# Two heads' value products merged, attention-weight remainders added by DMA, and the orders around them, in a two-layer encoder kernel

## The chip, the cores and the metric

The kernel runs on one core of one Trainium2 chip. The metric is the time of one execution on the device in microseconds. Three runs of the kernel before gave 1129.76, 1130.61 and 1131.30 us, median 1130.61 us.

The engines are named as in the profile: PE multiplies matrices (PEld loads its weights beside it), DVE and ACT work on tiles of 128 partitions and read PE's PSUM banks, POOL works on tiles in SBUF and can issue DMAs that add to what stands at the destination, SP issues the other DMAs.

## The reference, cut to what matters

Two layers over a sequence of 512 tokens with 1024 features, in float32. Layer 0 mixes tokens with latent attention (16 heads), layer 1 with an mLSTM (4 heads); behind each stands an FFN with 4096 hidden features.

```python
x += mla(rmsnorm(x));    x += ffn(rmsnorm(x), 0)
x += mlstm(rmsnorm(x));  x += ffn(rmsnorm(x), 1)

def mla(h):                                  # 16 heads
    cq  = rms_norm(h @ w_dq)                 # 512 x 384
    ckv = rms_norm((h @ w_dkv)[:, :256])     # 512 x 256, and 32 rotary columns
    q, k, v = cq @ w_uq, ckv @ w_ukv, ...    # per head 96 + (64 and 64)
    return softmax(mask(q @ k.T)) @ v @ w_o  # by heads, q and k normed, rotary

def mlstm(h):                                # 4 heads
    q, k, v, o = split(h @ w_in)             # v: 256 columns a head
    ...                                      # gates, decayed q k^T v, normed by row

def ffn(h, l): return square(relu(h @ w1[l])) @ w2[l]
```

## The kernel before, in words

**Numbers in two parts.** PE multiplies in f32r, a rounded form of float32. Every operand is therefore held as a rounded part hi and a remainder lo = raw - hi, and every product is three matmuls, hi*hi, hi*lo and lo*hi (`mm3`). A weight tile is loaded raw by DMA, ACT casts it to hi, and DVE (or POOL, or both by columns) subtracts to get lo (`split_w`, from line 155).

**Stages.** First comes `mla`. Its prologue computes the latents cq and ckv for four blocks of 128 tokens (tokens 0 to 3). The heads go in 8 pairs; each pair has one tile of weights, 128x1280 (`w_qkv`), split in `pair_w`: columns 0 to 767 on DVE, 768 to 1279 on POOL. Then follow the FFN of layer 0, the mLSTM, and the FFN of layer 1.

**What sets the order.** `ipe`, `idve`, `iact` and `ipool` keep what is issued through them in program order on their engine (all of it is recorded at line 80); what is issued through `nc.` directly, and ACT and POOL in most of `mla` and of the mLSTM, is placed by a scheduler when the kernel is built. In `mla` the program order is a list of two-letter units, written by hand. START is the prologue: W is a pair's weight split, R the transposes of a token block's latents, r their split, g, e and h the norm and the rotary part of the latents, P the product of a pair and a token block, A, B, C its squares, its scale and its scaled copy f, X the transposes of f, x their split. So "W10" is the second pair's weights and "P02" the first pair's product for token block 2. ORDER is one round of the heads in the middle, LAST the rounds of the last heads.

**The FFN.** The hidden features go in 8 chunks. A chunk's first product F gives z, squared; POOL makes four sums of z's quarters, ACT and DVE split them into hh and hl. The second product P uses seven products of sums of w2's quarters (a Strassen-Winograd form), (c,k) being chunk c and product k. The sums of the quarters are made by DMAs from POOL's queue that add to what was loaded. In the last chunk (7) all four sums t1 to t4 live in two tiles named z: `l_load` loads b12 four times, and `l_sum` (lines 804 to 806) adds b11 and b22 to t1 to t3, and b11, b22 and b21 to t4, one after another. It is called behind products k of chunk 6 (lines 936 to 942), whose order is 0, 1, 2, 3, 5, 4, 6. t4 feeds the very last product (7,6); its split is named zw. The adds of a finished product into x are DVE's `y_add`. The PSUM banks that they free are named tp. In layer 0, transposes that make the normed input xg of the mLSTM stand between the halves of the last two products; (7,5,0) and (7,5,1) are the two halves of product 5 of chunk 7.

**The mLSTM.** For each head, v is made with 256 (head 0: 264, with gates) columns a token block; the weights `w_v0`, and `w_v` for heads 1 to 3, are loaded raw in two tiles each, and those of head 0 are subtracted on POOL. `rows_sb` spreads a column of scales along the free axis: DVE writes them on diagonals, and one fp32 matmul with a matrix of ones gives the rows.

Of the kernel before, what the change touches and what calls it, by code (L numbers as in the profile page):

```python
# [16 lines left out]
F32 = mybir.dt.float32  # L17
F32R = mybir.dt.float32r
# [43 lines left out]
def trunk(ctx: ExitStack, tc, a, yT, dbg=None):  # L62
# [33 lines left out]
    def tmp(dt=F32):  # L96
        return ph[0].tile([P, 512], dt, tag="t", bufs=tb[0], name=nm("t"))
# [4 lines left out]
    def big(dt):  # L102
        return ph[0].tile([P, 4, 512], dt, tag="big", bufs=6, name=nm("big"))
# [84 lines left out]
    def rows(r):  # L188

        dg = tmp()  # L190
# [4 lines left out]
        return ps  # L195

    def rows_sb(r):
        ps = rows(r)
        R = ph[0].tile([P, T], F32, name=nm("R"))
        nc.scalar.copy(R, ps)  # L200
        return R
# [54 lines left out]
    def mla(mp):  # L256
# [101 lines left out]

        def new_pair(g):
            S = Pair()  # L360
            S.f, S.f2, S.ps, S.sps, S.tps, S.xps, S.mx = {}, {}, {}, {}, {}, {}, [None, None]
            S.p = [{}, {}]
            S.pT = [None, None]
            S.raw = load_raw(a["w_qkv"][g], PAIR_W)
            S.v = vt[g % 3]
            S.r = sp.tile([P, NB, 4], F32, tag="scr", bufs=4, name=nm("scr"))
            return S

        def pair_w(S):
            S.w = split_w(S.raw, PAIR_W, ENG[CFG[0]], ENG[CFG[1]], None if S is pairs[0] else ENG[CFG[4]], 3 * NQ,  # L370
                          [big(F32R).rearrange("p j e -> p (j e)") for _ in range(2)] if S is pairs[0] else None)

        pairs = {g: new_pair(g) for g in range(3)}
        gz = xtile()
# [206 lines left out]
        def o_split(S, h):  # L581
            o_sum(S, h)
            if h == 1:
# [4 lines left out]
                else:  # L588
# [9 lines left out]
        ORDER = ("S0 s0 P0 S1 S2 T0 X0 s1 T1 s2 D1 A0 T2 P1 M0 E0 t0 B0 t1 t2 E2 E3 A1 E1 V0 x0 X1 V1 V2 W0 V3 N0 C0 B1 x1 o0")  # L598

        START = ("W00 Z00 Z01 g00 e00 g01 Z02 R00 h00 r00 e01 Z04 g02 P00 R01 h01 A00 Z03 e02 r01 B00 W10 R02 g03 h02 C00 r02 P01 X00 A01 e03 R03 P02 B01 h03 r03 A02 C01 B02 P03 P10 x00 X01 C02 x01 A03 B03 X02 p11 x02 S01 C03 A10 P12 S00 X03 B10 W20 s01 A11 C10 X10 x03 s00 S02 A12 B11 s02 p13 M00 B12 C11 X11 x10 E00 E02 A13 B13 E01 E03 C12 N00 C13 x11")  # L600
# [122 lines left out]
    def ffn(fp, layer, last):  # L723
# [181 lines left out]
        for s_ in range(2, len(units) - 2):  # L905
# [80 lines left out]
    def mlstm(lp):  # L986
# [16 lines left out]
        def gates(gps):  # L1003
# [45 lines left out]
            nc.vector.tensor_scalar_mul(cs, r, DK ** -0.5)  # L1049
            G["cs"] = cs  # L1050

        for h in range(MH):
            nv = DV + (2 * MH if h == 0 else 0)
            src = a["w_v0"] if h == 0 else a["w_v"][h - 1]
            ws = [load_w(src[c], 4 * nv, nc.gpsimd if h == 0 else nc.vector) for c in range(2)]
            vh, vl = vt[2 * (h % 2)], vt[2 * (h % 2) + 1]
            nc.gpsimd.memset(vh.bitcast(F32)[:, :, DV:], 1.0)
            nc.gpsimd.memset(vl.bitcast(F32)[:, :, DV:], 0.0)
            gps = []
            for t in range(NB):  # L1060
# [7 lines left out]
                if h == 0 and t == 0:  # L1068
# [139 lines left out]
def _layout(i):  # L1208
# [13 lines left out]
    def rows_by_two(w):  # L1222
# [31 lines left out]
    o["w_v"] = np.stack([np.stack([cols(wv[:D // 2, h * DV:(h + 1) * DV]), cols(wv[D // 2:, h * DV:(h + 1) * DV])])  # L1254
                         for h in range(1, MH)])
# [24 lines left out]
```

## Time and profile before

| what | value |
|---|---|
| runs of before | 1129.76, 1130.61, 1131.30 us (median 1130.61) |
| the profiled execution | 1130.33 us, its span 1128.6 us |
| PE busy | 1107.3 us (98%) |
| DVE busy | 763.3 us (68%) |
| ACT busy | 568.0 us (50%) |
| POOL busy | 363.4 us (32%) |
| PE's longest waits | 2.4 us (for DVE's add into x), 1.9 us twice, 1.6 us |

The span is what the trace covers; the profiled execution's own time is 1.7 us longer. Shares of busy time are means over stages with different limits. PE's busy time is the sum of modelled spans of pipelined matmuls, so the distance between the starts of equal matmuls tells more than their duration. The granted clock, PEclk, is 1.00 at PE's 2.4 GHz and 0.50 at 1.2 GHz. A row's bracket gives the idle time of its engine just before it and what ended it.

### The profile page before, as it was taken

What the parts mean: (1) busy time and instruction counts of PE and PEld (TensorE: products, weight loads), DVE (VectorE), ACT (ScalarE), POOL (GpSimd) and SP (SyncE); (2) the same over time, 40 slices, a digit from 0 to 9 for tenths busy, and PEclk for the clock granted to TensorE, in tenths of its full rate; (3) what the DMA queues carried; (4) which work ended last, traced back from release to release, by engine and by line L of the source; (5) the groups of instructions that cost most, each with busy time, mean ns of one, the idle gap of its engine ahead of it and who ended that gap; (6) DMA issues with size and microseconds to landing.
All of it is one profiled execution on the core that took longest, in us unless ns stands there. A gap on an engine that the chain in (4) does not pass through costs nothing.

```text
span 1128.6 us, 15807 instructions
## 1 busy us (share of the span) xinstructions
PE 1107.3 (98%) x5790; PEld 949.1 (84%) x5790; DVE 763.3 (68%) x1308; ACT 568.0 (50%) x1004; POOL 363.4 (32%) x481
## 2 busy tenths in 40 slices
PE   9899999999999999999999999999999999999998
PEld 8889988888888888888798898888888888888876
DVE  5689997455676776776776465554476776767567
ACT  4478876437444544444465344332654545444442
POOL 3567785203332323324330011000323224224250
PEclk9899999999999999999999999999999999999999
DMA  9201021455666676575923223222675575666575
GB/s 323 72 25 48 20 76 38 131 170 127 170 151 149 165 154 146 151 174 149 203 71 102 86 58 92 81 90 81 197 170 130 159 180 131 164 168 139 160 153 127
DMA packets 44669, 146.23 MB, mean 130 GB/s; under 512 B 4912, under 2 KB 8368, under 8 KB 44592
## 3 DMA queue, kind: packets, MB, share of 16 engines
q1 hardware_dynamic: 34512, 108.52, 30.6%
q0 software_dynamic: 10080, 36.70, 19.2%
q8 instruction: 46, 0.75, 0.3%
q14 instruction: 31, 0.25, 0.1%
HBM read 143.11 MB, written 2.10 MB: 129 GB/s over the span
## 4 chain that ended last, share of the span: by engine, by line
PE 90%; DMA 3%; DVE 3%; POOL 2%; ACT 1%; issue 1%; SPq 0%; ACTq 0%; DVEq 0%; POOLq 0%
PE mm L80 40%; PE tp L80 34%; PE mm L178 4%; PE mm L177 4%; PE mm L176 4%; PE po L80 3%; DMA z<-in_w 1%; DMA wr<-in_w_z 1%; DVE x L80 1%; PE tp L178 1%; PE tp L177 1%; PE tp L176 1%; DMA t<-in_x 1%; POOL z L80 0%; POOL x L80 0%
## 5 line engine op out<-in xcount | busy, mean ns | idle before, releaser
L80 PE MATMUL mm<-xg,wh 128*128 128x512 f32 (+1 forms) x1088 | 318.9, 377 | 0.0
L80 POOL TENSOR_TENSOR z<-z 128x256 f32<-128x256 f32 x128 | 145.1, 1153 | 348.3 <-ACT z L80 345.8
L80 PEld LDWEIGHTS mm<-xg,wh 128*128 128x128 f32 x1088 | 200.1, 188 | 37.5
L80 PE MATMUL mm<-xg,wl 128*128 128x512 f32 (+1 forms) x544 | 204.9, 377 | 0.0
L80 DVE TENSOR_TENSOR wl<-tw,wh 128x1024 fp32r<-128x1024 f32 x104 | 134.5, 1293 | 87.9 <-ACT wh L80 87.9
L80 PE MATMUL tp<-wh,hh 128*128 128x512 f32 x424 | 165.3, 390 | 4.7 <-DVE x L80 4.7
L80 PE MATMUL tp<-wh,hl 128*128 128x512 f32 x424 | 165.0, 389 | 0.0
L80 PE MATMUL tp<-wl,hh 128*128 128x512 f32 x424 | 165.0, 389 | 0.0
L80 DVE TENSOR_TENSOR wl<-wr,wh 128x1024 fp32r<-128x1024 f32 (+1 forms) x72 | 94.0, 1306 | 102.1 <-ACT wh L80 102.1
L80 DVE SCALAR_TENSOR_TENSOR x<-tp,r,x 128x512 f32<-128x512 f32 (+1 forms) x223 | 155.2, 735 | 2.6 <-PE tp L80 2.5
L80 ACT ACTIVATE t<-mm 128x512 f32<-128x512 f32 (+3 forms) x97 | 54.3, 559 | 185.5 <-PE mm L80 179.5
L80 ACT CAST wh<-tw 128x1024 fp32r<-128x1024 f32 x104 | 108.9, 1047 | 40.5 <-DMA tw<-in_w 23.7
L80 PEld LDWEIGHTS mm<-xg,wl 128*128 128x128 f32 x544 | 102.4, 188 | 18.9 <-DVE wl L80 0.4
L80 PEld LDWEIGHTS tp<-wh,hh 128*128 128x128 f32 x424 | 79.6, 188 | 22.6 <-issue 3.5
L80 ACT CAST wh<-wr 128x1024 fp32r<-128x1024 f32 (+1 forms) x74 | 79.0, 1067 | 29.9 <-PE tp L80 25.5
L80 PEld LDWEIGHTS tp<-wh,hl 128*128 128x128 f32 x424 | 79.6, 188 | 16.6
L80 PEld LDWEIGHTS tp<-wl,hh 128*128 128x128 f32 x424 | 79.6, 188 | 16.5
L80 POOL DMA_DIRECT2D tw<-in_w x56 | 49.1, 876 | 124.4 <-DVE wl L80 112.4
L166 DVE TENSOR_TENSOR wl<-wr,wh 128x1024 fp32r<-128x1024 f32 (+1 forms) x39 | 45.7, 1173 | 56.3 <-ACT wh L162 55.5
L162 ACT CAST wh<-wr 128x1024 fp32r<-128x1024 f32 (+2 forms) x42 | 41.9, 1001 | 63.1 <-PE mm L177 31.6
L80 ACT ACTIVATE hh<-z 128x1024 fp32r<-128x1024 f32 x32 | 34.0, 1064 | 71.5 <-POOL z L80 71.5
L80 PE MATMUL mm<-wh,big 128*128 128x256 f32 (+1 forms) x256 | 58.2, 306 | 0.0
(286 smaller groups left out, 2096.5 us busy)
## 6 DMA issues: line engine op xcount, KB each, us to landing
wr<-in_w SPq DMA_DIRECT2D x64, 512.0 KB, 3.7
tw<-in_w SPq DMA_DIRECT2D x62, 512.0 KB, 4.2
tw<-in_w POOLq DMA_DIRECT2D x56, 512.0 KB, 5.7
z<-in_w POOLq DMA_DIRECT2D x14, 512.0 KB, 7.7
wr<-in_w_qkv SPq DMA_DIRECT2D x8, 640.0 KB, 3.9
wr<-in_w_oa SPq DMA_DIRECT2D x8, 512.0 KB, 3.6
z<-in_w SPq DMA_DIRECT2D x8, 512.0 KB, 7.3
wr<-in_w_mo SPq DMA_DIRECT2D x8, 512.0 KB, 3.6
```

What stands on the lines that cost most here:

```text
L80: return lambda *args, **kw: tc.keep_in_program_order(f(*args, **kw)) if self.on else f(*args, **kw)
L162: act.copy(hi[:, :n], raw[:, :n])
L166: dve.tensor_sub(lo[:, :n], raw[:, :n], hi[:, :n].bitcast(F32))
L176: pe.matmul(out, lhsT=lh, rhs=rh, start=start, stop=False)
L177: pe.matmul(out, lhsT=lh, rhs=rl, start=False, stop=False)
L178: pe.matmul(out, lhsT=ll, rhs=rh, start=False, stop=stop)
```

## The change

It does six things.

1. Pairs 3 to 7 of the attention weights: ACT writes lo as the negated rounded weights, a DMA from POOL's queue adds the raw weights (640 KB) to it, and ACT casts hi. Pairs 0 to 2 are split as before.
2. Units are moved in START, ORDER and LAST: "W10" goes from before R02 to behind "h02 e03", P01 and P02 come ahead of R03 and X00, and W0 goes to an earlier place in two lists.
3. `l_sum`: t4's b11 is added behind the z sums and behind t2's b22, and t4's b22 behind that.
4. The remainders of `w_v0`, two subtractions of 128x1056, are made on DVE.
5. v of heads 2 and 3 is one product with 512 columns: 96 matmuls of 512 columns for 192 of 256, from four tiles of weights, in four PSUM banks.
6. `rows_sb` splits the scales into two rounded parts and uses two f32r matmuls.

```diff
     def pair_w(S):
-        S.w = split_w(S.raw, PAIR_W, ENG[CFG[0]], ENG[CFG[1]], None if S is pairs[0] else ENG[CFG[4]], 3 * NQ,
...
+        if S.g < 3:
+            S.w = split_w(S.raw, PAIR_W, iact, idve, None if S.g == 0 else ipool, 3 * NQ,
...
+            return
+        hi, lo = S.w = [wp.tile([P, WMAX], F32R, tag=n, name=nm(n)) for n in ("wh", "wl")]
+        iact.activation(lo[:, :PAIR_W], S.raw[:, :PAIR_W], AF.Copy, scale=-1.0)
+        ipool.dma_start(lo[:, :PAIR_W], a["w_qkv"][S.g], accum_op=add)
+        iact.copy(hi[:, :PAIR_W], S.raw[:, :PAIR_W])
...
-  START = ("... P00 R01 h01 A00 Z03 e02 r01 B00 W10 R02 g03 h02 C00 r02 P01 X00 A01 e03 R03 P02 B01 ...
+  START = ("... P00 R01 h01 A00 Z03 e02 r01 B00 R02 g03 r02 C00 P01 h02 e03 W10 A01 P02 R03 X00 B01 ...
...
                     elif k == 3:
-                        l_sum(("t1", "b11"), ("t2", "b11"), ("t3", "b22"), ("t4", "b11"))
+                        l_sum(("t1", "b11"), ("t2", "b11"), ("t3", "b22"))
                     elif k == 5:
                         s_load(c + 1, ("b21", "b22"))
-                        l_sum(("t2", "b22"), ("t4", "b22"))
+                        l_sum(("t2", "b22"), ("t4", "b11"))
+                    elif k == 4:
+                        l_sum(("t4", "b22"))
                     elif k == 6:
                         l_sum(("t4", "b21"))
...
-            ws = [load_w(src[c], 4 * nv, nc.gpsimd if h == 0 else nc.vector) for c in range(2)]
+                ws = [load_w(src[c], 4 * nv) for c in range(2)]
...
+            if h == 2:
+                z = [ps_mm() for _ in range(3)] + [pp.tile([P, 512], F32, tag="po", bufs=1, name=nm("po"))]
+                for j in range(4):
+                    w = load_w(a["w_v23"][j], D)
+                    for t in range(NB):
+                        for k in (2 * j, 2 * j + 1):
+                            o_mm(z[t], w, k, t, xg)
...
+    def rows_sb(r):
+        rh, rl = small(NB), small(NB)
+        nc.vector.tensor_copy(rh.bitcast(F32R), r)
+        nc.vector.tensor_sub(rl, r, rh)
+        dh, dl = tmp(F32R), tmp(F32R)
         for t in range(NB):
-            nc.vector.tensor_scalar_mul(dg[:, t * P:(t + 1) * P], ident, r[:, t:t + 1])
+            c = slice(t * P, (t + 1) * P)
+            nc.vector.tensor_scalar_mul(dh[:, c], ident, rh[:, t:t + 1])
+            nc.scalar.activation(dl[:, c], ident, AF.Copy, scale=rl[:, t:t + 1])
         ps = ps_tp()
-        pe.matmul(ps, lhsT=ones, rhs=dg, start=True, stop=True)
+        pe.matmul(ps, lhsT=ones_r, rhs=dh, start=True, stop=False)
+        pe.matmul(ps, lhsT=ones_r, rhs=dl, start=False, stop=True)
```

Three places in the engines' lists. The first is DVE's list in the prologue of `mla`, around token block 2's split, before: `wl` is the second pair's remainder, `z_ue` the latents' norm, `f` the scaled first pair of token block 0, `big` and `ck` the remainders of the turned latents of block 2, `x` the scaled latents of block 3.

```order
L80 TENSOR_TENSOR wl_587<-wr_369,wh_586 128x768
L80 TENSOR_SCALAR z_ue<-z_ms,rx_390 128x3
L80 SCALAR_TENSOR_TENSOR f_582<-mm_527,scr_368,qtab 128x128 x2
L80 TENSOR_TENSOR f_582<-mm_527,scr_368 128x2x64
L80 TENSOR_TENSOR big_214<-tp_591,big_213 128x3x128
L80 TENSOR_TENSOR big_214<-tp_592,big_213 128x128
L80 TENSOR_TENSOR ck_216<-tp_592,ck_215 128x128
L80 SCALAR_TENSOR_TENSOR x_649<-tp_222,z_ab,x_375 128x384
```

The same place now:

```order
L80 TENSOR_SCALAR z_ue<-z_ms,rx_390 128x3
L80 TENSOR_TENSOR big_214<-tp_586,big_213 128x3x128
L80 TENSOR_TENSOR big_214<-tp_587,big_213 128x128
L80 TENSOR_TENSOR ck_216<-tp_587,ck_215 128x128
L80 SCALAR_TENSOR_TENSOR f_582<-mm_527,scr_368,qtab 128x128 x2
L80 TENSOR_TENSOR f_582<-mm_527,scr_368 128x2x64
L80 SCALAR_TENSOR_TENSOR x_634<-tp_222,z_ab,x_375 128x384
L80 SCALAR_TENSOR_TENSOR x_634<-tp_222,r_388,x_375 128x32
L80 SCALAR_TENSOR_TENSOR x_635<-po_223,z_ab,x_377 128x256
L80 TENSOR_TENSOR wl_640<-wr_369,wh_639 128x768
```

The weights' remainder went from the front of this part to its end, and the split of block 2 ahead of `f`.

The second place is the last adds into x at the end of layer 0's FFN on DVE, before: `x_3191` and `x_3195` are the second feature half of token blocks 0 and 1, `zw_5869` and `zw_5886` the remainders for the products (7,5) and (7,6), `tp_5797` and `tp_5798` the two banks.

```order
L80 TENSOR_TENSOR zw_5869<-z_5649,zw_5869 128x1024
L80 SCALAR_TENSOR_TENSOR x_3191<-tp_5797,r_737_3422,x_3191 128x512
L80 SCALAR_TENSOR_TENSOR x_3195<-tp_5798,r_737_3422,x_3195 128x512
L80 TENSOR_TENSOR zw_5886<-z_5649,zw_5886 128x1024
L80 SCALAR_TENSOR_TENSOR x_3191<-tp_5817,r_737_3422,x_3191 128x512
L80 SCALAR_TENSOR_TENSOR x_3195<-tp_5818,r_737_3422,x_3195 128x512
L80 SCALAR_TENSOR_TENSOR x_3199<-tp_5797,r_737_3422,x_3199 128x512
```

The same place now, with `wl_6024` and `wl_6030`, the remainders of the two `w_v0` tiles:

```order
L80 TENSOR_TENSOR zw_5869<-z_5649,zw_5869 128x1024
L80 SCALAR_TENSOR_TENSOR x_3191<-tp_5797,r_737_3422,x_3191 128x512
L166 TENSOR_TENSOR wl_6024<-wr_6021,wh_6023 128x1056
L80 SCALAR_TENSOR_TENSOR x_3195<-tp_5798,r_737_3422,x_3195 128x512
L80 TENSOR_TENSOR zw_5886<-z_5649,zw_5886 128x1024
L166 TENSOR_TENSOR wl_6030<-wr_6027,wh_6029 128x1056
L80 SCALAR_TENSOR_TENSOR x_3191<-tp_5817,r_737_3422,x_3191 128x512
L80 SCALAR_TENSOR_TENSOR x_3195<-tp_5818,r_737_3422,x_3195 128x512
L80 SCALAR_TENSOR_TENSOR x_3199<-tp_5797,r_737_3422,x_3199 128x512
```

Two subtractions came in, the first between the adds that free the two banks. On ACT the cast of the first tile, `wh_6023`, stands right behind the cast of `zw_5886`, as before.

The third place is POOL's list there, before: `z_5646` holds t1 and t2, `z_5649` t3 and t4, `z_5642` is the last z.

```order
L80 DMA z_5646<-in_w 128x1024 x2
L80 DMA z_5649<-in_w 128x1024 x2
L80 TENSOR_TENSOR z_5642<-z_5642 128x256 x4
L80 DMA z_5646<-in_w 128x1024
L80 DMA z_5649<-in_w 128x1024 x2
L166 TENSOR_TENSOR wl_6024<-wr_6021,wh_6023 128x1056
```

The same place now:

```order
L80 DMA z_5646<-in_w 128x1024 x2
L80 DMA z_5649<-in_w 128x1024
L80 TENSOR_TENSOR z_5642<-z_5642 128x256 x4
L80 DMA z_5646<-in_w 128x1024
L80 DMA z_5649<-in_w 128x1024 x3
L166 TENSOR_TENSOR wl_6247<-wr_6244,wh_6246 128x1024
```

One of t4's additions went behind the z sums, so that all three stand in a row there, and the subtractions of `w_v0` are gone.

## Rows read from the trace of the kernel before

**Rows 1.** The page's busy table, PE: busy us (share) x instructions.

```profile
PE 1107.3 (98%) x5790; PEld 949.1 (84%) x5790; DVE 763.3 (68%) x1308; ACT 568.0 (50%) x1004; POOL 363.4 (32%) x481
```

**Rows 2.** PE's waits: engine line <- awaited: us, times, longest us.

```profile
PE tp L80 <- DVE x L80: 4.7, 4, 2.4
```

**Rows 3.** PE's timeline in the prologue: start us, us, instruction, count [idle before].

```profile
44.75 0.73 PE L80 MATMUL tp<-cst,f 128*128 128x128 f32 x2 [1.94 <-DVE f L80]
```

**Rows 4.** Stretches: busy us of PE, PEld, DVE, ACT, POOL; PEclk, DMA share, GB/s.

```profile
45.00:51.80 6.80, 4.87 (x23) 4.57 (x23) 4.59 (x16) 1.78 (x6) 4.87 (x19) 0.50 0.30 96
...
1100.00:1104.00 4.00, 3.09 (x14) 2.57 (x15) 4.00 (x7) 0.78 (x2) 0.00 (x0) 1.00 0.96 184
```

**Rows 5.** Timelines of ACT, DVE and POOL in the prologue.

```profile
40.91 1.27 ACT L80 CAST wh<-wr 128x1280 fp32r<-128x1280 f32 x1
...
43.52 0.92 DVE L80 TENSOR_SCALAR z_ue<-z_ms,rx 128x3 f32<-128x3 f32 x1 [0.35 <-ACT t L80]
...
43.15 1.26 POOL L80 TENSOR_TENSOR wl<-wr,wh 128x512 fp32r<-128x512 f32 x1
```

**Rows 6.** Timelines of DVE and PE around 160 us.

```profile
154.66 1.29 DVE L80 TENSOR_SCALAR sm<-sm 128x4 f32<-128x4 f32 x1
...
158.05 0.94 DVE L80 TENSOR_TENSOR wl<-wr,wh 128x768 fp32r<-128x768 f32 x1
...
164.57 0.66 PE L80 MATMUL tp<-cst,x 128*128 128x128 f32 x4 [1.63 <-DVE sm L80]
```

**Rows 7.** PE's timeline: 256 columns in the prologue, 512 columns in the mLSTM.

```profile
52.03 1.60 PE L80 MATMUL mm<-big,big 128*128 128x256 f32 x12
53.46 0.52 PE L80 MATMUL mm<-big,ck 128*128 128x256 f32 x3
...
597.68 0.39 PE L177 MATMUL mm<-xg,wh 128*128 128x512 f32 x1
...
599.72 0.39 PE L177 MATMUL mm<-xg,wh 128*128 128x512 f32 x1
```

**Rows 8.** PE's timeline, the matmul of `rows_sb`.

```profile
600.31 1.10 PE L194 MATMUL tp<-t,ones 128*128 128x512 f32 x2
```

**Rows 9.** Timelines of ACT, POOL, DVE and PE, end of layer 0's FFN.

```profile
546.53 0.63 ACT L80 ACTIVATE z<-t 128x512 f32<-128x512 f32 x1
...
548.05 4.85 POOL L80 TENSOR_TENSOR z<-z 128x256 f32<-128x256 f32 x4
...
555.74 0.86 POOL L80 DMA_DIRECT2D z<-in_w  x1 [2.03 <-DMA z<-in_w]
561.41 0.86 POOL L80 DMA_DIRECT2D z<-in_w  x1 [4.81 <-DMA z<-in_w]
...
566.80 1.05 ACT L80 CAST zw<-z 128x1024 fp32r<-128x1024 f32 x1 [2.99 <-DMA z<-in_w]
...
568.75 1.21 DVE L80 TENSOR_TENSOR zw<-z,zw 128x1024 fp32r<-128x1024 f32 x1
...
571.49 0.71 PE L80 MATMUL tp<-zw,hh 128*128 128x512 f32 x2
...
574.19 0.71 PE L80 MATMUL tp<-zw,hh 128*128 128x512 f32 x2
```

**Rows 10.** Timelines of ACT, POOL and PE, end of layer 1's FFN.

```profile
1090.21 0.63 ACT L80 ACTIVATE z<-t 128x512 f32<-128x512 f32 x1
...
1097.69 1.77 POOL L80 DMA_DIRECT2D z<-in_w  x2
1106.13 0.86 POOL L80 DMA_DIRECT2D z<-in_w  x1 [6.66 <-DMA z<-in_w]
...
1100.91 0.47 PE L80 MATMUL tp<-wh,hh 128*128 128x512 f32 x1 [2.41 <-DVE x L80]
...
1119.06 0.71 PE L80 MATMUL tp<-zw,hh 128*128 128x512 f32 x2
```

**Rows 11.** The page's DMA issues: count, KB each, median us to landing.

```profile
wr<-in_w SPq DMA_DIRECT2D x64, 512.0 KB, 3.7
```

More of the change, by code (lines that the diff above doesn't have):

```diff
@@ L186, in proj @@
             mm3(out, hi[:, c], lo[:, c], rhs[k][0], rhs[k][1], k == 0, k == n - 1)
-    def rows(r):
-        dg = tmp()
+    def rows_sb(r):
[3 more added lines that the diff above has]
+        dh, dl = tmp(F32R), tmp(F32R)
         for t in range(NB):
-            nc.vector.tensor_scalar_mul(dg[:, t * P:(t + 1) * P], ident, r[:, t:t + 1])
+            c = slice(t * P, (t + 1) * P)
+            nc.vector.tensor_scalar_mul(dh[:, c], ident, rh[:, t:t + 1])
+            nc.scalar.activation(dl[:, c], ident, AF.Copy, scale=rl[:, t:t + 1])
         ps = ps_tp()
-        pe.matmul(ps, lhsT=ones, rhs=dg, start=True, stop=True)
-        return ps
-    def rows_sb(r):
-        ps = rows(r)
+        pe.matmul(ps, lhsT=ones_r, rhs=dh, start=True, stop=False)
+        pe.matmul(ps, lhsT=ones_r, rhs=dl, start=False, stop=True)
         R = ph[0].tile([P, T], F32, name=nm("R"))
@@ L360, in new_pair @@
             S = Pair()
+            S.g = g
             S.f, S.f2, S.ps, S.sps, S.tps, S.xps, S.mx = {}, {}, {}, {}, {}, {}, [None, None]
@@ L369, in pair_w @@
         def pair_w(S):
-            S.w = split_w(S.raw, PAIR_W, ENG[CFG[0]], ENG[CFG[1]], None if S is pairs[0] else ENG[CFG[4]], 3 * NQ,
-                          [big(F32R).rearrange("p j e -> p (j e)") for _ in range(2)] if S is pairs[0] else None)
+            if S.g < 3:
+                S.w = split_w(S.raw, PAIR_W, iact, idve, None if S.g == 0 else ipool, 3 * NQ,
+                              [big(F32R).rearrange("p j e -> p (j e)") for _ in range(2)] if S.g == 0 else None)
+                return
[3 more added lines that the diff above has]
+            iact.copy(hi[:, :PAIR_W], S.raw[:, :PAIR_W])
         pairs = {g: new_pair(g) for g in range(3)}
@@ L597, in mla @@
                  "T": p_bank, "t": p_split, "V": pv, "o": o_split}
-        ORDER = ("S0 s0 P0 S1 S2 T0 X0 s1 T1 s2 D1 A0 T2 P1 M0 E0 t0 B0 t1 t2 E2 E3 A1 E1 V0 x0 X1 V1 V2 W0 V3 N0 C0 B1 x1 o0")
-        START = ("W00 Z00 Z01 g00 e00 g01 Z02 R00 h00 r00 e01 Z04 g02 P00 R01 h01 A00 Z03 e02 r01 B00 W10 R02 g03 h02 C00 r02 P01 X00 A01 e03 R03 P02 B01 h03 r03 A02 C01 B02 P03 P10 x00 X01 C02 x01 A03 B03 X02 p11 x02 S01 C03 A10 P12 S00 X03 B10 W20 s01 A11 C10 X10 x03 s00 S02 A12 B11 s02 p13 M00 B12 C11 X11 x10 E00 E02 A13 B13 E01 E03 C12 N00 C13 x11")
+        ORDER = ("S0 s0 P0 S1 S2 T0 X0 s1 T1 s2 W0 D1 A0 T2 P1 M0 E0 t0 B0 t1 t2 E2 E3 A1 E1 V0 x0 X1 V1 V2 V3 N0 C0 B1 x1 o0")
+        START = ("W00 Z00 Z01 g00 e00 g01 Z02 R00 h00 r00 e01 Z04 g02 P00 R01 h01 A00 Z03 e02 r01 B00 R02 g03 r02 C00 P01 h02 e03 W10 A01 P02 R03 X00 B01 h03 r03 A02 C01 B02 P03 P10 x00 X01 C02 x01 A03 B03 X02 p11 x02 S01 C03 A10 P12 S00 X03 B10 W20 s01 A11 C10 X10 x03 s00 S02 A12 B11 s02 p13 M00 B12 C11 X11 x10 E00 E02 A13 B13 E01 E03 C12 N00 C13 x11")
         PRO = {"Z": lambda t: z_mm((((0, 0), (0, 1)), ((1, 0), (1, 1)), ((2, 1), (3, 1)), ((3, 0),), ((2, 0),))[t], range(KD - ZL, KD)), "e": z_out, "R": z_turn, "Q": lambda t: z_turn(t, True), "r": z_split,
@@ L1050, in gates, with v_out @@
             G["cs"] = cs
+        def v_out(h, t, ps):
+            vh, vl = vt[2 * (h % 2)], vt[2 * (h % 2) + 1]
+            nc.scalar.activation(vh[:, t, 0:DV], ps, AF.Copy, scale=r[:, t:t + 1])
+            nc.vector.scalar_tensor_tensor(vl[:, t, 0:DV], ps, r[:, t:t + 1], vh.bitcast(F32)[:, t, 0:DV],
+                                           op0=mult, op1=sub)
         for h in range(MH):
-            nv = DV + (2 * MH if h == 0 else 0)
-            src = a["w_v0"] if h == 0 else a["w_v"][h - 1]
-            ws = [load_w(src[c], 4 * nv, nc.gpsimd if h == 0 else nc.vector) for c in range(2)]
             vh, vl = vt[2 * (h % 2)], vt[2 * (h % 2) + 1]
-            nc.gpsimd.memset(vh.bitcast(F32)[:, :, DV:], 1.0)
-            nc.gpsimd.memset(vl.bitcast(F32)[:, :, DV:], 0.0)
+            if h < 2:
+                nv = DV + (2 * MH if h == 0 else 0)
+                src = a["w_v0"] if h == 0 else a["w_v1"]
+                ws = [load_w(src[c], 4 * nv) for c in range(2)]
+                nc.gpsimd.memset(vh.bitcast(F32)[:, :, DV:], 1.0)
+                nc.gpsimd.memset(vl.bitcast(F32)[:, :, DV:], 0.0)
             gps = []
-            for t in range(NB):
+            for t in range(NB) if h < 2 else ():
                 tk = slice(t * P, (t + 1) * P)
@@ L1075, in mlstm @@
                     roots(1)
-                nc.scalar.activation(vh[:, t, 0:DV], ps[:, 0:DV], AF.Copy, scale=r[:, t:t + 1])
-                nc.vector.scalar_tensor_tensor(vl[:, t, 0:DV], ps[:, 0:DV], r[:, t:t + 1],
-                                               vh.bitcast(F32)[:, t, 0:DV], op0=mult, op1=sub)
+                v_out(h, t, ps[:, 0:DV])
                 if h == 0:
@@ L1082, in mlstm @@
                     gps.append(gs)
+            if h == 2:
[5 more added lines that the diff above has]
+                            o_mm(z[t], w, k, t, xg)
+                for t in range(NB):
+                    for n in range(2):
+                        v_out(2 + n, t, z[t][:, n * DV:(n + 1) * DV])
             if h == 0:
@@ L1253, in _layout @@
     o["w_v0"] = np.stack([cols(v0[:D // 2]), cols(v0[D // 2:])])
-    o["w_v"] = np.stack([np.stack([cols(wv[:D // 2, h * DV:(h + 1) * DV]), cols(wv[D // 2:, h * DV:(h + 1) * DV])])
-                         for h in range(1, MH)])
+    o["w_v1"] = np.stack([cols(wv[:D // 2, DV:2 * DV]), cols(wv[D // 2:, DV:2 * DV])])
+    o["w_v23"] = wv[:, 2 * DV:].reshape(4, 2, P, 512).transpose(0, 2, 1, 3).reshape(4, P, D)
     o["w_mo"] = tiles(w_in[:, 2 * hq + hv:])
```

2 lines of the change are left out of this document (1 added, 1 removed).

## The prediction, made before the change was run

> **What bounds the kernel now.** I read the page's busy table first, then PE's waits, then PE's own rows at each wait, and last the granted clock by stretch. PE is busy for 98% of the span [rows 1], so only two things can move the time: PE's own work, and the few places where PE stands still. Its waits are led by DVE's adds into x, 4.7 us in 4 waits, most of it at the ends of the two FFNs [rows 2]. The profiled execution took 1130.33 us, 1.7 us more than its span of 1128.6 us; the sum is made on that time, and the median of the runs, 1130.61 us, is 0.3 us above it. All clock times below are those of the trace of before.
>
> **The prologue.** PE stands still for 1.9 us before 44.75 [rows 3], and there are waits like it some 3 us and some 19 us later; from 45.0 to 51.8 its granted clock is 0.50, so it runs at 1.2 GHz, and 4.87 us of matmuls cost it twice their time [rows 4]. What it waits for comes late because the second pair's weight split stands ahead of it: on POOL the 1.26 us subtraction at 43.15, and DVE's z_ue waits for ACT's squares until 43.52, which stand behind the 1.27 us cast on ACT [rows 5]. The new START puts that split behind token 2's transposes. Following the new order by hand with the old durations: z_ue is done at about 42.7 in place of 44.4, the lows of token 2 at 44.3, P02 runs at 44.3, R03 and X00 from 46.2, P03 at 49.0, P10 at 50.7, and X01 at 52.6 where it was 55.6. The waits some 19 us later shift and stay, since their chain starts from X02 and is the same. That is -3.0 us if the clock does not fall. PE still has two idle stretches of 1.5 to 1.7 us there, so it may fall: bounds 0 and -5 (the first wait gone twice over, and half of the 4.87 us at 1.2 GHz given back); I take -2.8.
>
> **Pair weights by DMA.** For each of five pairs DVE loses 768 columns (0.94 us) [rows 6] and POOL 512 columns (1.26 us, as in [rows 5]); ACT gains a second pass over 1280 columns (1.27 us, as in [rows 5]), and POOL the issue of a DMA, under 1 us. The raw weights are in SBUF tens of microseconds before they are used, so an addition of 640 KB has time to land. In the repeated part of MLA PE has no wait, so neither gain nor cost shows there; ACT has room, and I bound its extra pass by 0 and +1.5 us in all, and take 0. The one place where it can pay is the wait of 1.63 us at 164.57, released by DVE [rows 6]. DVE has hardly any idle time ahead of it; there it does the 0.94 us subtraction at 158.05, and a 4-column op at 154.66 that took 1.29 us beside a POOL subtraction. The first goes, and POOL's 1024-column subtraction beside the second is now issued earlier. I take -1.5 us, from 0 to -2.
>
> **v of heads 2 and 3.** 192 matmuls of 256 columns become 96 of 512. Twelve 256-column matmuls start in 1.43 us (52.03 to 53.46), 0.119 each; nine intervals of 512 columns take 2.04 us (597.68 to 599.72), 0.227 each [rows 7]. So 22.9 us become 21.8: -1.1 us (0 to -1.5; the four banks are free early in the head's order). The Trainium skill, "TensorE: Matmul & The Clock Gate", section "Back-to-back issue gap", gives columns/2.4 + 2.5 ns for a single gap; by that the merge would save only about 0.25 us, but the rows show 10 ns more for each of either kind, and their difference is what counts here.
>
> **The row of scales.** The fp32 matmul is 1.10 us in its two passes [rows 8], some of it beside its neighbour; two f32r matmuls take 2 x 0.227 = 0.45. That is at most -0.65 us, and I take -0.5 (0 to -0.65); DVE's two and ACT's four small ops stand beside PE's work.
>
> **The end of layer 0's FFN.** This is the largest term, and it goes the other way. Before, t4's first addition, b11, is issued ahead of POOL's four z subtractions and runs beside them; b22 is issued at 555.74, b21 at 561.41, and ACT can cast t4 at 566.80, so each of the last two takes 5.4 to 5.7 us from issue to release [rows 9]. In the new order nothing of t4 starts before the z subtractions end and t2's b22 has been issued. ACT's square that they need ends at 547.16 and they take 4.85 us, from 548.05 before [rows 9]; now they can end near 552.0, where t2's b22 is issued, and t4's b11 at 552.9. The second of two such additions 0.88 us apart released POOL 7.56 us after its issue in layer 1 (1098.57 to 1106.13) [rows 10]. So b11 is in at 560.5, b22 at 566.1, b21 at 571.5: 4.7 us later than before.
> Before, that would have held up only the last product. Now DVE's list has the subtraction of the first w_v0 tile between two adds into x (x_3191 and x_3195, see the second list of the change), and its ACT cast stands behind t4's cast. So: t4's cast 571.5 to 572.6, w_v0's cast until 573.5, DVE's subtraction (1.25 us, scaled from 1.21 for 1024 [rows 9]) until 574.75, x_3195 until 575.5, and only then is PE's bank for (7,5,1) free. PE starts it at 575.6 where it was 571.49: 4.1 us. Behind it DVE does t4's subtraction, the second w_v0 tile, three adds and two evictions, until about 580.7, and (7,6,0) starts near 581.1 where it was 574.19 [rows 9]. That is +6.9 us, and v follows it as before. POOL's split of these two tiles, which goes, was beside PE's work. Bounds: with each addition at 5.4 us t4 lands at 569.2 and the loss is +4.9; if t4 were not late at all, two subtractions on a full DVE still cost +2.4.
> PE would stand still there for 3.9, 1.8 and 1.1 us within 9 us. After the prologue's idle stretch the clock fell to 1.2 GHz; around a single wait of 2.41 us at 1100.91 the granted clock stayed at 1.00, 2.4 GHz [rows 4, 10]. The new place looks more like the first: 0 to +2.5 us, I take +1.2.
>
> **The end of layer 1's FFN.** There ACT's square ends at 1090.84, and t2's b22, right behind the z subtractions, is issued at 1097.69, so these began some 2 us behind the square [rows 10]. They no longer wait behind t4's b11, which takes most of the 2.41 us wait at 1100.91; but the last product waits for t4, now by the same sum in at 1115.4 where it was 1111.7. There is no w_v0 here. With its cast, subtraction and three adds the last product's first half starts at about 1119.8 where it was 1119.06 [rows 10]: +0.7 (-1.5 to +1.5).
>
> **Sum.** -2.8 - 1.5 - 1.1 - 0.5 + 6.9 + 1.2 + 0.7 = +2.9 us; 1130.33 + 2.9 = 1133.2, and with the 0.3 us to the median 1133.5 us.
>
> **Rivals.**
> A. The blocked DVE list costs little, because t4 lands in time. For it: a plain load of 512 KB lands in 3.7 us [rows 11], and with additions near that t4 would be in at about 565. Then the layer-0 end costs +2.4, layer 1 gives about -1.3, and the clock stays: -5.9 + 2.4 - 1.3 = -4.8, about 1126 us. Against it: all additions in the rows take 5.4 us or more. The Trainium skill, "DMA: Bandwidth & Descriptors", section "Anatomy of one DMA — SWDGE (gpsimd) path", gives 2.0 us + bytes/436e3 for a DMA of this path, 3.2 us for 512 KB, by which this rival would hold; the rows of this case disagree with it (5.4 to 5.7 us), and the measurement decides. With 5.4 us each (+4.9, clock up) the same sum ends at about 1130.
> B. The prologue gives more: no fall of the clock at all, some -6 in place of -2.8. For it: PE's work is now more even there. Against it: the chain behind X02 and its waits are as before. About 1130 us.
> C. Worse: PE at 1.2 GHz through the end of layer 0's FFN and into v, +2.5 in place of +1.2, the prologue's clock falls as before (gain near 0), and ACT's extra passes delay x0's banks by 0.3 us a pair, +1.5: about 1139 us. It decides from the point where ACT's queue is late at a bank that PE needs next.
> D. The move does not do what it says: z starts when it did, since ACT's squares and not t4's load release it. Then t4 is 0.85 us later still and layer 1 loses 2 us: about 1136 us.
>
> **How the numbers follow.** Forecast 0.50 (own range 1130.5 to 1136.5), A 0.23 (1126, a part of it near 1130), B 0.10, C and D 0.17. A measurement of this kernel tells about 0.2% (2.3 us) from no change. Faster by more than that, below 1128.35: most of A and a part of B, 0.27. Within: the lower part of the forecast, the rest of A and B, 0.21. Slower, above 1132.9: the rest of the forecast, C and D, 0.52. The range 1125 to 1139 us reaches from A to C.
>
> **What would show it.** In the profile after: POOL's three t4 issues in a row behind t2's b22, some 5.4 to 7.6 us apart; DVE idle for a few microseconds between x_3191 and x_3195 with ACT's w_v0 cast as releaser; PE waiting for DVE x about 4 us before (7,5,1) in layer 0; X01 of the prologue about 3 us earlier; no wait at 164; 96 matmuls of 512 columns for the last two heads' v. The prediction is wrong if PE passes from (7,5,0) to (7,5,1) in layer 0 without a wait of over 2 us, or if t4 is cast at its old distance from the z subtractions.

## The result, and the profile after

The changed kernel takes 1140.01 us (median of 4 runs, 1138.40 to 1141.78) where the kernel before takes 1130.95 us in the same sessions: a ratio of 1.0077, 95% interval 1.0062 to 1.0092, that is 8.7 us slower (7.0 to 10.4). 1133.5 us was predicted, and 1125 to 1139 as the range: the direction is right, the size is not, and the time lies outside of the range. The span of its profiled execution, the shortest of the four, is 1136.6 us, 8.0 us longer than before.

Where the time went is best read from PE: the same matmul stands in both traces, and the difference of its starts, counted along the program, says in which stretch the time was lost. The table is worked out from such pairs of starts (before, after).

| stretch, up to PE's matmul at | shift there | change in the stretch | predicted |
|---|---|---|---|
| prologue (68.64, 66.51) | -2.1 | -2.1 | -2.8 |
| rest of attention, FFN of layer 0 but its end (552.43, 554.37) | +1.9 | +4.1 | -1.5 |
| end of layer 0's FFN (576.28, 585.60) | +9.3 | +7.4 | +8.1 |
| mLSTM and the FFN of layer 1 but its end (1095.51, 1103.52) | +8.0 | -1.3 | -1.6 |
| end of layer 1's FFN (1124.24, 1132.33) | +8.1 | +0.1 | +0.7 |

One stretch is off by 5.6 us, the others by less than 1 us each. At PE's matmul at 29.98 us, where the two kernels' lists do not differ yet, the shift is already +0.55 us, so the new START's own part of the first row is -2.7 us. PE's waits after (columns as in [rows 2]):

```profile
PE tp L80 <- DVE x L80: 7.5, 6, 4.5
PE tp L80 <- DVE sm L80: 3.2, 4, 0.8
PE tp L80 <- DVE f L80: 2.6, 3, 1.4
PE mm L80 <- DVE x L80: 2.0, 3, 1.2
```

Two of them tell the story: the waits for DVE's adds into x have a member of 4.5 us that was not there, and the one long wait for sm of [rows 6] has become four of about 0.8 us.

**Attention.** These are the timelines of ACT, DVE and PE around one of the four waits, in the changed kernel:

```profile
86.04 1.28 ACT L80 ACTIVATE wl<-wr 128x1280 fp32r<-128x1280 f32 x1
87.20 0.49 ACT L80 ACTIVATE t<-mm 128x384 f32<-128x384 f32 x1
...
87.71 1.30 ACT L80 CAST wh<-wr 128x1280 fp32r<-128x1280 f32 x1
88.88 0.62 ACT L80 CAST big<-tp 128x512 fp32r<-128x512 f32 x1
...
87.73 0.55 DVE L80 TENSOR_REDUCE sm<-t 128x2 f32<-128x192 f32 x2 [0.87 <-ACT t L80]
89.53 0.69 DVE L80 TENSOR_TENSOR big<-tp,big 128x512 fp32r<-128x512 f32 x1 [1.06 <-ACT big L80]
...
91.80 0.66 PE L80 MATMUL tp<-cst,f 128*128 128x128 f32 x4 [0.81 <-DVE sm L80]
```

ACT now makes two passes over the pair's weights, 1.28 and 1.30 us, with a squares pass between them; behind them stands the cast of big, DVE waits 1.06 us for it, everything on DVE behind that is late, and PE waits for the last of it, the maxima (sm) of the scores that free its bank. The same place before, on ACT and DVE:

```profile
87.76 1.29 ACT L80 CAST wh<-wr 128x1280 fp32r<-128x1280 f32 x1
88.92 0.62 ACT L80 CAST big<-tp 128x512 fp32r<-128x512 f32 x1
...
89.57 0.69 DVE L80 TENSOR_TENSOR big<-tp,big 128x512 fp32r<-128x512 f32 x1 [0.23 <-ACT big L80]
```

DVE waited for this cast already, by 0.23 us. So ACT had no room there: it was busy with the softmax and the casts in one row up to this cast. Of the 1.28 us put in front of it, 0.97 us came through as a slip of PE's starts, here and again near 110 and 129 us.

**The end of layer 0's FFN.** POOL, ACT, DVE and PE, to be held against [rows 9]:

```profile
549.51 4.63 POOL L80 TENSOR_TENSOR z<-z 128x256 f32<-128x256 f32 x4 [2.67 <-ACT z L80]
554.09 1.77 POOL L80 DMA_DIRECT2D z<-in_w  x2
562.39 0.86 POOL L80 DMA_DIRECT2D z<-in_w  x1 [6.54 <-DMA z<-in_w]
568.36 0.86 POOL L80 DMA_DIRECT2D z<-in_w  x1 [5.11 <-DVE x L80]
...
574.13 1.04 ACT L80 CAST zw<-z 128x1024 fp32r<-128x1024 f32 x1 [8.40 <-DMA z<-in_w]
575.08 1.07 ACT L162 CAST wh<-wr 128x1056 fp32r<-128x1056 f32 x1
...
576.17 1.26 DVE L166 TENSOR_TENSOR wl<-wr,wh 128x1056 fp32r<-128x1056 f32 x1 [6.11 <-ACT wh L162]
577.35 0.75 DVE L80 SCALAR_TENSOR_TENSOR x<-tp,r,x 128x512 f32<-128x512 f32 x1
...
578.15 1.22 PE L80 MATMUL tp<-zw,hh 128*128 128x512 f32 x2 [4.51 <-DVE x L80]
...
583.69 0.71 PE L80 MATMUL tp<-zw,hh 128*128 128x512 f32 x2
```

This is the predicted sequence step by step: three additions to t4 in a row (7.4, 6.0 and 5.8 us from issue to release), t4's cast 7.3 us later than in [rows 9] where PE was 1.9 us late, w_v0's cast and subtraction behind it, x_3195 and then PE, after a wait of 4.51 us. Three stretches show the clock; the columns are those of [rows 4]:

```profile
45.00:52.00 7.00, 5.31 (x39) 4.51 (x39) 5.98 (x19) 3.11 (x9) 6.56 (x19) 1.00 0.25 95
61.00:66.00 5.00, 4.36 (x18) 3.76 (x19) 4.39 (x19) 1.85 (x7) 3.96 (x7) 0.66 0.63 190
...
578.00:581.40 3.40, 3.25 (x9) 2.56 (x10) 3.40 (x5) 2.02 (x4) 2.03 (x1) 0.50 0.54 154
```

Early in the prologue the granted clock now stays at 1.00 where [rows 4] had 0.50. Its second fall there is not gone: from 61 to 66 us the mean is 0.66, where before it was 0.64 from 66 to 70 us. Behind the 4.51 us wait it is 0.50, 1.2 GHz, for 3.4 us.

**The mLSTM.** One matmul of the merged v and the one seven further on, and the first of the two f32r matmuls of the scales, where [rows 8] had 1.10 us:

```profile
689.81 0.39 PE L177 MATMUL mm<-wl,xg 128*128 128x512 f32 x1
...
691.40 0.40 PE L178 MATMUL po<-wh,xg 128*128 128x512 f32 x1
...
610.74 0.47 PE L199 MATMUL tp<-t,ones_r 128*128 128x512 f32 x1
```

Seven intervals of 512 columns take 1.59 us (689.81 to 691.40), 0.227 each, as forecast. By PE's shifts the scales give 0.4 us and the merge 1.15 us.

### The profile page after: what moved, and what is told of

Same layout as the page of the kernel before. It is cut to its first block, busy times and chain, and to the rows that moved or that the text cites. A ratio compares the mean times of both kernels' runs of the same rounds, so it can differ in the third digit from the quotient of the medians.

```text
span 1136.6 us, 15618 instructions
## 1 busy us (share of the span) xinstructions
PE 1108.6 (98%) x5694; PEld 943.1 (83%) x5694; DVE 758.9 (67%) x1307; ACT 573.9 (50%) x1013; POOL 356.8 (31%) x475
## 4 chain that ended last, share of the span: by engine, by line
PE 82%; issue 4%; POOL 4%; ACT 3%; DMA 3%; DVE 3%; SPq 0%; POOLq 0%; ACTq 0%; DVEq 0%
PE mm L80 37%; PE tp L80 30%; PE mm L178 3%; PE mm L176 3%; PE mm L177 3%; PE po L80 2%; POOL z L80 1%; ACT x L80 1%; DMA z<-in_w 1%; DMA wr<-in_w_z 1%; DVE x L80 1%; POOL scr L80 1%; POOL wl L80 1%; PE tp L178 1%; PE tp L177 1%
## 5 line engine op out<-in xcount | busy, mean ns | idle before, releaser
L80 DVE TENSOR_TENSOR wl<-wr,wh 128x1024 fp32r<-128x1024 f32 (+1 forms) x67 | 88.6, 1322 | 101.7 <-ACT wh L80 101.7
L166 DVE TENSOR_TENSOR wl<-wr,wh 128x1024 fp32r<-128x1024 f32 (+2 forms) x41 | 48.3, 1177 | 56.5 <-ACT wh L162 56.0
```

The costliest lines, as they stand in the source:

```text
L80: return lambda *args, **kw: tc.keep_in_program_order(f(*args, **kw)) if self.on else f(*args, **kw)
L166: dve.tensor_sub(lo[:, :n], raw[:, :n], hi[:, :n].bitcast(F32))
```

## The experiments

In all of them the ratio is to the kernel before, run beside them; 0.001 is 1.13 us. Twelve kernels ran.

### Pairs 3 to 7 split as before

```diff
-            if S.g < 3:
+            if S.g < 8:
```

> The changed kernel with the weights of pairs 3 to 7 split as before (cast on ACT, subtractions on DVE and POOL); all else as changed. Theory: ACT's second pass of 1.28 us stands ahead of a cast that PE's next bank needs, five times about 1 us. Then the waits for DVE sm near 91.8, 110.5 and 129.2 us (0.97 us each) go, attention ends some 5 us earlier, and the time is about 1135 us (ratio to before 1.0035). Rival: the waits come from W0's new place in the list and from the new prologue; then the time stays at 1139 to 1141 us.

Ratio 1.0049 (1.0036 to 1.0062), 3.2 us faster than the changed kernel. The waits near 91.8, 110.5 and 129.2 are gone (0.97 us is the slip of PE's starts at each; the rows show 0.81 us of idle time), so the theory's mechanism holds, but the gain is smaller than 5 us: PE's starts slip by 0.4 to 0.6 us at four places instead, and by 1.4 us near 158, where PE waits 1.2 us for DVE's tri; DVE's subtraction now stands at W0's new place. By PE's shifts from 68.64 to 185 us attention gains 2.0 us. Both sides were partly right, which made W0's place a suspect of its own.

### w_v0 on POOL again

```diff
-                ws = [load_w(src[c], 4 * nv) for c in range(2)]
+                ws = [load_w(src[c], 4 * nv, nc.gpsimd if h == 0 else nc.vector) for c in range(2)]
```

> The changed kernel with the two remainders of w_v0 on POOL again. Theory: the end of layer 0's FFN loses 7.4 us by two things together, t4's late additions and the w_v0 subtraction that waits for them between two adds on DVE. With the subtractions gone PE no longer waits 4.5 us before (7,5,1), the clock stays at 1.00, and the last product still waits for t4: about 4.5 us less, 1135.5 us. Rival: only the subtractions' own 2.4 us go, and PE waits as long before (7,6,0): about 1137.6 us.

Ratio 1.0060 (1.0047 to 1.0072), 1.9 us faster, with intervals that overlap. The theory falls, and the rival is right in that PE waits further on: PE passes (7,5,1) without the long wait and then waits 1.5 us for DVE's adds and 2.7 us for xg. By PE's shifts the end of layer 0's FFN costs as much as in the changed kernel, and the clock falls all the same (0.50 from 579.6 to 583.5 us). ACT, DVE and PE of this run:

```profile
572.64 1.05 ACT L80 CAST zw<-z 128x1024 fp32r<-128x1024 f32 x1 [8.22 <-DMA z<-in_w]
...
575.81 2.00 ACT L162 CAST wh<-wr 128x1056 fp32r<-128x1056 f32 x2
577.72 2.28 ACT L80 ACTIVATE xg<-mm,cst 128x256 fp32r<-128x256 f32 x6
...
578.57 0.88 DVE L80 SCALAR_TENSOR_TENSOR xg<-mm,cst,xg 128x256 fp32r<-128x256 f32 x2 [1.64 <-ACT xg L80]
...
579.60 1.09 PE L80 MATMUL mm<-cst,x 128*128 128x128 f32 x4 [2.72 <-DVE xg L80]
```

ACT's evictions into xg stand behind t4's cast, with the casts of `w_v0` and other work between, as they do in the changed kernel; and DVE's adds stand behind t4's subtraction at 573.73. With t4 late there is more than one way to PE, and closing one of them left the others.

### t4's additions at their old places

```diff
-                        l_sum(("t1", "b11"), ("t2", "b11"), ("t3", "b22"))
+                        l_sum(("t1", "b11"), ("t2", "b11"), ("t3", "b22"), ("t4", "b11"))
                     elif k == 5:
                         s_load(c + 1, ("b21", "b22"))
-                        l_sum(("t2", "b22"), ("t4", "b11"))
-                    elif k == 4:
-                        l_sum(("t4", "b22"))
+                        l_sum(("t2", "b22"), ("t4", "b22"))
```

> The changed kernel with t4's three additions at their old places; w_v0 stays on DVE. Theory: t4 can be cast some 5 us earlier, so the subtraction of w_v0 between the adds starts at about 570.5 in place of 576.2, and the end of layer 0's FFN costs about 2.4 us more than before in place of 7.4: 1135 us, layer 1's end unchanged within 1 us. Rival: DVE's order is the whole cost, and the time falls by less than 1.5 us.

Ratio 0.9995 (0.9986 to 1.0004): 9.3 us faster than the changed kernel, more than expected. The two traces differ by 6.7 us, since the profiled execution of the changed kernel is the shortest of its runs (1138.40 us). By the shifts of PE 1.7 us of these lie up to 185 us, which this edit does not touch (PE's wait of 1.1 us for tri near 151 in the changed kernel is missing here); 3.9 us lie from there to the end of layer 0's FFN and 1.8 us in the end of layer 1's, which I had taken as neutral; 0.7 us go the other way in between. Such waits come and go from kernel to kernel, and their cause stays open. Behind PE's matmul at 565.91, where t4 and w_v0 act, the cost over the kernel before is 2.2 us, near the 2.4 that the theory gave.

### Both of these

The two edits above together.

> The changed kernel with both undone, w_v0 on POOL and t4's additions at their old places. Theory: the end of layer 0's FFN costs what it did before, 7.4 us less than in the changed kernel, about 1132.5 us; what is left over before is attention's loss of 2 us less the gain of the merge. Rival: a part of the 7.4 us comes from elsewhere (the merged v's order, or the earlier loads of w_v), and the time stays above 1134 us.

Ratio 0.9978 (0.9969 to 0.9987), 11.2 us faster than the changed kernel and some 4 us faster than the theory gave. The rival is out. The four kernels form a square. By the ratios t4's place is worth 9.3 us with w_v0 on either engine (1.0077 to 0.9995, 1.0060 to 0.9978), and w_v0's engine 1.9 us with t4 at either place, which would mean that the two add up. The traces show that at the end of layer 0's FFN they do not. The growth of PE's shift from its matmul at 565.91 us of the kernel before to the one at 594.96 us, in the mLSTM:

| | w_v0 on DVE | w_v0 on POOL |
|---|---|---|
| t4's additions late | +7.4 us | +7.4 us |
| t4's additions at their old places | +2.2 us | +0.1 us |

t4's place is the cost: with w_v0 on POOL its 9.3 us are 7.2 us here and 2.3 us at the end of layer 1's FFN. With t4 early, w_v0's two subtractions on a full DVE cost 2 us; with t4 late they cost nothing more, since PE is held as long without them. The 1.9 us that the ratio gives for w_v0 with t4 late are within its intervals, and the traces of the two kernels do not have them at this place.

### One pass on ACT, the DMA kept

```diff
-            iact.copy(hi[:, :PAIR_W], S.raw[:, :PAIR_W])
+            idve.tensor_copy(hi[:, :PAIR_W], S.raw[:, :PAIR_W])
```

> The changed kernel with the additions by DMA kept for pairs 3 to 7, but hi cast on DVE in place of ACT, so that ACT makes one pass of 1.28 us a pair as before. Theory: ACT's second pass is what costs; then the waits of 0.97 us near 91.8, 110.5 and 129.2 go and the time falls by 3 to 4 us (ratio to before about 1.0045). Rival: the DMA costs, by its issue on POOL or its traffic; then these waits stay and the ratio stays near 1.0077.

Ratio 1.0047 (1.0035 to 1.0060), 3.4 us faster than the changed kernel, as the theory expected: the DMAs are all there, and the three waits for sm are gone. So at W0's new place ACT's second pass is what PE felt, not the DMA.

### Pairs, w_v0 and t4 as before; lists, merge and scales as changed

The edits of the first and the fourth experiment together.

> Pairs split as before, w_v0 on POOL and t4's additions at their old places; left of the change are the lists START, ORDER and LAST, the merged v and the f32r scales. Theory: the two costs add up, so it is 2 to 3 us faster than the run that undid w_v0 and t4 alone (0.9978): ratio about 0.9955. Rival: without the DMA the DVE subtractions at W0's new place bring waits of their own (0.38 us a round, and 1.4 us near 158 in the run with the pairs split), and the ratio is 0.997 or more.

Ratio 0.9976 (0.9967 to 0.9985): the same as with the DMA (0.9978). The rival is right. At W0's new place the old split costs about what the new one costs: PE's starts slip by 0.4 to 0.6 us a round, and by 1.4 us near 158, where it waits for tri.

### The z sums first, then t4, then t2

```diff
-                        l_sum(("t1", "b11"), ("t2", "b11"), ("t3", "b22"), ("t4", "b11"))
+                        l_sum(("t1", "b11"), ("t2", "b11"), ("t3", "b22"))
                     elif k == 5:
                         s_load(c + 1, ("b21", "b22"))
-                        l_sum(("t2", "b22"), ("t4", "b22"))
+                        l_sum(("t4", "b11"), ("t2", "b22"))
+                    elif k == 4:
+                        l_sum(("t4", "b22"))
```

> As the run of this call with pairs split, w_v0 on POOL and the old additions, but with the z sums ahead of t4's b11, and t4's b11 issued ahead of t2's b22 behind them. Theory: ACT's evictions into xg stand behind t4's cast, so what counts is when t4 is in; it is in 2.3 us later in layer 0 and 1.2 us later in layer 1, and the time is 1 to 2.5 us longer than in that run. Rival: the earlier z sums win back their 0.9 and 2 us and the time is the same or less.

Ratio 0.9986 (0.9977 to 0.9995), 1.1 us slower than the experiment ahead of it, with intervals that overlap. By the time alone it points the theory's way and is not shown. By PE's shifts the end of layer 0's FFN does cost 2.6 us more than in the experiment ahead of it (+2.8 in place of +0.2, between the matmuls at 565.91 and 594.96), near the theory's 2.3, but the end of layer 1's costs nothing more (-1.8 in both), where the theory had 1.2.

### START as changed, ORDER and LAST of before

Pairs, w_v0 and t4 as before as well; W0 is back behind V2 in ORDER and behind V0 in the first part of LAST.

```diff
-  ORDER = ("S0 s0 P0 S1 S2 T0 X0 s1 T1 s2 W0 D1 A0 T2 ... V0 x0 X1 V1 V2 V3 N0 C0 B1 x1 o0")
+  ORDER = ("S0 s0 P0 S1 S2 T0 X0 s1 T1 s2 D1 A0 T2 ... V0 x0 X1 V1 V2 W0 V3 N0 C0 B1 x1 o0")
```

> As the run of this call with pairs split, w_v0 on POOL and the old additions, but with ORDER and LAST of before: W0 at its old place, START as changed. Theory: the prologue's gain of about 2 us was lost again in the middle of attention by W0's earlier place, which puts DVE's subtraction ahead of the adds that PE waits for; with W0 back it is kept: 2 to 2.5 us faster than that run, ratio about 0.994. Rival: W0's place costs nothing and the two are the same within 0.5 us.

Ratio 0.9947 (0.9934 to 0.9959), 1125.61 us: 3.3 us faster than with ORDER and LAST as changed, and faster than both kernels, 6.0 us less than the kernel before. W0's new place was a cost. The shift of PE is -2.2 us at 73.7 and still about that at 552, so the prologue's gain now lasts through attention.

### The same with the DMA at W0's old place

The test is `S.g < 3` again in the kernel ahead of this one.

> The fastest run so far (ratio 0.9947: START as changed, ORDER and LAST of before) with the additions by DMA for pairs 3 to 7, so with W0 at its old place. Theory: W0 had to go to an earlier place because a DMA takes over 5 us to land there and the pair's first product follows some 4 us behind the cast; at the old place PE waits 2 to 4 us for each of five pairs, and the ratio is about 1.005 to 1.010. Rival: it lands in time, only ACT's second pass counts (under 1 us a pair), and the ratio is 0.996 to 0.999.

Ratio 0.9991 (0.9982 to 1.0000), 5.0 us slower than the kernel without the DMA. My theory was wrong: nothing waits for the DMA, and the rival is nearer, the ratio just past the upper edge of its range. PE's waits without the DMA and with it, each from its own run:

```profile
PE tp L80 <- DVE f L80: 1.7, 2, 1.4
PE tp L80 <- DVE sm L80: 1.6, 1, 1.6
```

```profile
PE tp L80 <- DVE sm L80: 3.2, 4, 0.8
...
PE tp L80 <- DVE f L80: 2.7, 3, 1.4
```

One wait has become four, three of them where the changed kernel had them, and the waits for f grow from 1.7 us to 2.7 by one near 71, behind the first two of the extra passes. The price of the new split, all else equal, is 5.0 us for five pairs by the ratios, and 3.2 us by the spans of the two traces (1123.8 and 1127.0 us). With the earlier runs this makes a second square. The change of PE's shift from its matmul at 29.98 us of the kernel before to the one at 185.04, START as changed in all four:

| | W0 at its old place | W0 at its new place |
|---|---|---|
| old split | -4.2 us | -0.4 us |
| DMA and two passes on ACT | +0.5 us | +0.5 us |

The changed kernel itself, the same as the last of them up to here, has +1.7 us, so these numbers are good to about 1 us. Either change alone costs 4 to 5 us in attention, and both together no more than the split alone.

### And with hi cast on DVE

> As the run with the DMA at W0's old place, but hi cast on DVE. Theory: ACT is not what PE waits for there but the DMA, so it is within 1.5 us of that run. Rival: ACT's second pass is, and it is 3 us or more faster than that run.

Ratio 0.9998 (0.9988 to 1.0007), within the 1.5 us of the theory but for another reason than it gave: the three waits for sm are gone, and PE instead waits 3.2 us once for sm near 164, and its starts slip by 0.5 to 0.6 us at four places. So at this place of W0 the cost of the split does not hang on ACT's second pass alone: it goes to other waits when the pass goes to DVE. The trace shows why the wait near 164 is twice as long. Ahead of sm DVE makes another remainder, 128x1024, and in this run POOL makes one at the same time; the third line is DVE's in the run without the cast on DVE:

```profile
160.32 2.74 DVE L80 TENSOR_TENSOR wl<-wr,wh 128x1024 fp32r<-128x1024 f32 x1
159.59 2.38 POOL L80 TENSOR_TENSOR wl<-wr,wh 128x1024 fp32r<-128x1024 f32 x1
...
162.49 1.24 DVE L80 TENSOR_TENSOR wl<-wr,wh 128x1024 fp32r<-128x1024 f32 x1
```

DVE's subtraction took 1.5 us longer beside POOL's.

### Merge and scales alone

START, ORDER, LAST, pairs, w_v0 and t4 as before.

> The kernel before with only the merged v and the f32r scales (START, ORDER, LAST, pair weights, w_v0 and the additions as before). Theory: 1.1 us for the merge and 0.5 to 0.7 us for the scales, with no new wait: ratio about 0.9985, so that START's 2.2 us are the rest of the 0.9947. Rival: the merge alone brought most of it, and the ratio is 0.996 or less.

Ratio 0.9970 (0.9960 to 0.9981), 3.4 us where 1.7 were expected. In the shifts of PE the mLSTM gives 1.6 us of it, as forecast. The rest lies where nothing was edited: 0.7 us by 552, and 0.8 us at the end of layer 1's FFN, where PE waits 1.4 and 0.6 us in place of 0.5 and 2.4. START's gain is the step from this kernel to 0.9947, 2.6 us.

### The merge alone

The scales as before as well.

> The kernel before with only the merged v. Merge and f32r scales together gave a ratio of 0.9970 (3.4 us) where 1.6 to 1.8 us were expected. Theory: the merge saves its 1.1 us and the scales their 0.5 to 0.7, and what is over is a shorter wait at the end of layer 1's FFN that has no cause in either; the ratio is 0.9975 to 0.999. Rival: the scales carry the surplus, and the merge alone is at 0.999 or above.

Ratio 0.9977 (0.9968 to 0.9986), 2.6 us, inside the theory's bounds: the merge's part in the mLSTM is 1.1 us by the shifts (-0.3 to -1.4), and the same shorter wait at the end of layer 1's FFN shows again. In its profile l_load lands sooner against POOL's queue than in that of before; why is open, and it concerns 0.8 us.

## Why the prediction was wrong, and where it was right

1. **What bounds the kernel: right.** The loss is in places where PE stands still, and in 3.4 us at 1.2 GHz behind one of them.
2. **The prologue: right.** -2.8 forecast, -2.1 by the shifts in the changed kernel (-2.7 from 29.98 us on), -2.6 from the merge-and-scales kernel to the one with the new START. From 45 to 52 us the clock stayed up; its second fall stayed, as the waits ahead of it were forecast to.
3. **Pair weights by DMA: this step failed.** It said "ACT has room, and I bound its extra pass by 0 and +1.5 us in all, and take 0", and took -1.5 us at the wait near 164. I had looked for PE's waits, found none in the repeated part, and read from that that the engines behind PE had slack. They had almost none: before, DVE already waited 0.23 us for the very cast that stands behind the new pass. At W0's old place the new split costs 5.0 us for five pairs by the ratios and 3.2 by the traces. With W0 moved as well, the cost over the kernel that kept the old split and the old place is 3.5 us (0.9947 to 0.9978); that the move wins a part of the split's cost back is not shown, as 0.9991 and 0.9978 overlap and both traces have +0.5 us. Against the -1.5 taken these 3.5 make 5.0 of the 6.5 us by which the forecast missed. Of the wait near 164 (1.63 us in [rows 6]) 0.8 us are left, but as much is left with the old split at W0's new place, where PE comes to it 1.4 to 1.6 us later than before; so the gain forecast for the split is not shown at all. That DVE's subtraction at that place goes was right; that PE would have the time of it was not.
4. **W0's place was not priced at all.** The prediction named the move only where it hides a POOL subtraction. With the old split the new place alone costs 3.3 us (0.9947 to 0.9976). It puts 1.3 us on ACT and 0.9 us on DVE at an earlier point of the round, and PE then waits for DVE's tri; which of the two holds tri was not tested.
5. **The end of layer 0's FFN: right in size, by a way to PE that is not the only one.** +8.1 forecast, +7.4 by the shifts, and every step of the chain is in the trace: t4 4.7 us late by the sum and 5.4 us by the trace, PE's wait 4.51 us, the clock at 1.2 GHz behind it. But the prediction made w_v0's subtraction between the adds the thing that turns t4's delay into PE's. The square of four kernels says otherwise: without it the same stretch costs the same 7.4 us, as t4's subtraction on DVE and ACT's evictions behind t4's cast hold PE as well. I had followed one subtraction in DVE's list, and not ACT's list. That two subtractions on a full DVE cost 2.4 us when t4 is not late was nearly right: 2.2 us. (The lower bound of +4.9 should have been +4.6, 2.3 us less than the +6.9; nothing hangs on it.)
6. **The end of layer 1's FFN: nearly right.** +0.7 forecast and +0.1 seen, in part by luck: with the old additions in the changed kernel the same stretch is 1.8 us shorter than in the profile of before, which had a longer wait there (2.41 us) than any later run with these additions. Against those the late additions cost 1.8 us, and the step was some 1 us too small.
7. **Merge and scales: right.** -1.6 forecast; in the mLSTM -1.6 by the shifts after, and -1.6 in the kernel with these alone (-1.3 after, when the FFN of layer 1 up to its end is counted in).
8. **The rivals.** A and B are out. C came nearest in time, 1139 us, by luck in its sum: one of its three mechanisms is the one that decided, ACT's extra pass at a bank that PE needs next, but it put it at 0.3 us a pair, beside two others that did not come (the prologue's gain stayed, and the clock was down for 3.4 us only), and gave it little chance. D is out: the z sums began 0.08 us behind ACT's square.

## What to carry to other kernels

That PE has no wait in a stretch does not say that the engines behind it have room. Before putting a pass on one, read its own list at that place and look for who waits for its next instruction, if only by 0.2 us: from there on most of the pass can come through, as 0.97 of 1.28 us did here. And price a move of old work to a new place like new work: W0's place alone cost as much as most of the split. When a late buffer is found, follow every in-order queue that has an instruction on it, since work queued behind that instruction is as late as the buffer, and freeing one queue shows the next. And before two causes are added up, look at the stretch where both act: here each cost 2 and 7 us alone, and both 7.

## What the runs showed of the hardware

An addition of 512 KB by DMA, issued from POOL 0.9 us behind another, took 7.4 us from its issue to the next release in the changed kernel, and 5.8 to 6.0 us with no other addition beside it; in [rows 9, 10] it was 7.6 and 5.4 to 5.7. In the changed kernel the granted clock was 0.50 for 3.4 us behind PE's wait of 4.51 us, and 0.50 from 63 to 66 us behind two waits of 1.4 and 0.6 us that ended at 61.02 and 62.22; it stayed at 1.00 at the waits of 0.8 and 0.6 us at 554.37 and 557.96. A subtraction of 1024 columns on DVE took 2.74 us with one of POOL's beside it for 1.6 us, and 1.24 us in a run without POOL's.
